# Re-planned issue order in a multi-query attention kernel: earlier value products, planned value scalings, another start and end

## The chip, the cores and the metric

The kernel runs on one core of a Trainium2 chip. The metric is the device time of one execution in microseconds (us). TensorE is called PE here, its weight loads PEld, VectorE is DVE, ScalarE is ACT, GpSimd is POOL and SyncE is SP. The program has one core, so there is no second die to compare with.

## The reference, cut to what matters

```python
batch, seq_len, embed_dim = (8, 1024, 1024); num_heads = 16; head_dim = 64
# q: (8, 1024, 16, 64), k and v: (8, 1024, 64): one key and value head for all query heads
scores = np.matmul(q, k.transpose(0, 1, 3, 2)) / np.sqrt(head_dim)
weights = np.exp(scores - np.max(scores, axis=-1, keepdims=True))
weights = weights / np.sum(weights, axis=-1, keepdims=True)
attn_out = np.matmul(weights, v)
```

## The kernel before

The work is cut into 64 pairs of heads (8 per batch), and a pair into 8 key tiles of 128 keys. A key tile has two halves of 512 queries. For each half, PE makes scores for both heads (a "score product", two matmuls), then one engine turns them into weights, then PE multiplies weights and values (the "value products").

The exponential is the expensive part, and two engines share it. ACT does most tiles, one instruction of 128x1024 per half. Some tiles go to DVE, which builds the exponential from bit operations and products as a sum of three terms: two instructions `z` (one per half) and four further steps per tile. The three terms need three copies of the values, scaled by constants ("value scalings", three DVE instructions per batch). A DVE tile therefore also costs PE three times the value products.

What each engine does next is decided when the kernel is built. A function `plan` simulates PE, ACT and DVE with a handful of durations and emits the order of operations, which the program then follows. These are its constants, and the parts that the change touches (`...` marks a cut; most comments are added here):

```python
ACT_P, ACT_L = 0.905, 1.19                 # pace and latency of one ACT exponential, us
MARGIN, WAIT = 0.318, 0.153
END, END_LAG = 2.388, -0.293
BACKLOG, BACK_END = 4.816, 2.496           # how much DVE work may be open for one more DVE tile
LAST, SPLIT = 10, 3                        # no DVE tile in the last 10; the last 3 go half by half
WBUFS = 26
ZBUFS = 5
LAG = 1.355                                # value products trail scores by this many pairs
...
            lag = min(LAG, END_LAG + (LAG - END_LAG) * rest / END)
            av = tav <= T + (SWITCH if mode != "av" else 0) and (
                nv < 3 * NKT * (nq / (2 * NKT) - lag) or nq == 2 * NT
            )
...
    def begin(w):                          # called with the first score product of pair w
        ...
        if w == 1:
            scale_v(0)                     # three DVE instructions that plan() knows nothing of
        ...
            if hp == HP - 3:
                trans_k(b + 1)
                scale_v(b + 1)
...
        turn_first(0)                      # first halves of the first keys and queries, transposed on PE
        for n, (_, _, (op, *args)) in enumerate(order):
            if n == 2:
                turn_first(1)              # second halves, after two score products
            if op == "qk":
                ...
                score(*args)
```

The softmax here doesn't subtract the row's maximum and nothing guards it: scores larger than these inputs give would overflow.

## Time and profile before

The median of the first three runs is 763.41 us (763.12 to 763.8).

| | before |
|---|---|
| exponentials on ACT, pace | 812, 0.917 us |
| start of the first, end of the last | 7.01 us, 755.56 us |
| time lost in gaps between them | 4.15 us |
| from there to the end of the span | 5.70 us |

The pace is the median distance between the ends of successive exponentials in the trace. "Time lost in gaps" is the sum of what these distances exceed 0.9165 us by, over the 14 that do so by more than 0.025 us. With 1.02 us for the first exponential alone, 811 x 0.9165 = 743.3 us for the others and the rows of the table, 7.01 + 1.02 + 743.3 + 4.15 + 5.70 adds to 761.2 us of a span of 761.27 us. This sum is the budget in which the change is judged.

The page of the kernel before starts with the span and with busy time by engine (share of the span, number of instructions).

```profile
span 761.3 us, 29601 instructions
PE 731.3 (96%) x13648; PEld 485.3 (64%) x13648; DVE 728.3 (96%) x1050; ACT 747.6 (98%) x814; POOL 44.6 (6%) x61
```

ACT is the busiest, but PE and DVE are close, so a busy share alone does not settle which one bounds. Three of the groups of instructions of the same page follow. The columns are line, engine, operation, output and input, count, then busy time, mean ns of one, then idle time just before them and what ended most of it.

```profile
L432 ACT ACTIVATE w<-sc 128x1024 f16<-128x1024 f32 x812 | 745.7, 1295 | 3.8 <-PE sc L420 3.3
L446 DVE TENSOR_SCALAR z<-sc 128x1024 uint16<-128x1024 f32 x212 | 258.4, 1219 | 13.3 <-PE sc L420 10.1
L328 DVE TENSOR_SCALAR vals<-vn 128x512 f16<-128x512 f32 x24 | 8.7, 419 | 0.0
```

An exponential lasts 1.3 us on average in the record but they follow each other every 0.917 us, because neighbours overlap. The timeline of ACT of the kernel before shows the idle stretches; the columns are start, duration of the merged stretch, what ran, and in brackets the idle time before it and who ended it.

```profile
7.01 1.02 ACT L432 ACTIVATE w<-sc 128x1024 f16<-128x1024 f32 x1 [0.97 <-PE sc L420]
9.10 12.94 ACT L432 ACTIVATE w<-sc 128x1024 f16<-128x1024 f32 x14 [1.07 <-PE sc L420]
22.55 1.02 ACT L432 ACTIVATE w<-sc 128x1024 f16<-128x1024 f32 x1 [0.51 <-PE sc L420]
23.85 3.03 ACT L432 ACTIVATE w<-sc 128x1024 f16<-128x1024 f32 x3 [0.28 <-PE sc L420]
27.31 728.25 ACT L432 ACTIVATE w<-sc 128x1024 f16<-128x1024 f32 x793 [0.43 <-PE sc L420]
```

After 27.3 us the stretch of 793 exponentials looks unbroken, but the ends of single instructions show six losses of 0.13 to 0.25 us hidden in it and three smaller ones, 1.25 us together. Around 22 us the timelines of DVE and PE say who was late. First DVE:

```profile
19.02 1.09 DVE L328 TENSOR_SCALAR vals<-vn 128x512 f16<-128x512 f32 x3
20.03 0.69 DVE L459 TENSOR_SCALAR m<-z 128x2048 uint16<-128x2048 uint16 x1
20.63 1.22 DVE L446 TENSOR_SCALAR z<-sc 128x1024 uint16<-128x1024 f32 x1
```

Then PE, where score matmuls and the first value matmuls alternate:

```profile
21.90 1.03 PE L420 MATMUL sc<-qt,k2t 64*128 64x512 f16 x4 [1.03 <-DVE z L446]
22.87 0.40 PE L476 MATMUL acc<-vals,w 128*128 128x65 f16 x4
23.20 0.61 PE L420 MATMUL sc<-qt,k2t 64*128 64x512 f16 x2
25.58 0.52 PE L476 MATMUL acc<-vals,e 128*128 128x65 f16 x6
```

PE waited 1.03 us for the DVE exponential that stood behind the scalings. Besides, PE was slow here: score matmuls last about 0.6 us until 24.7 us, and 0.386 us later (median from 26.7 to 39.7 us). The trace, asked for the score line from 6.3 to 26.4 us, gives the shortest, median and longest in ns:

```profile
L420 PE MATMUL sc<-qt,k2t x50: 580/604/631, 6.4 to 24.7; 64*128 64x512 f16 x50
```

The trace's record of the granted clock begins only at 26.44 us, with the full clock, and the first fast score matmul starts at 26.67 us. So this phase is called PE's slow clock here, and its end the release. The granted-clock row does not show it: it reads 1.00 for 7 to 28 us of the kernel before, where score matmuls lasted 604 ns until 24.7 us. The matmul durations do.

### The profile page before, as it was taken

How to read it: one execution, taken by the hardware profiler on the slowest of the kernel's cores; microseconds unless marked ns; L12 is line 12 of the kernel's file. 1: busy time of each engine (PE TensorE's matmuls, PEld its weight loads, DVE VectorE, ACT ScalarE, POOL GpSimd, SP SyncE). 2: the span in 40 equal slices, each digit the busy share in tenths (PEclk: the TensorE clock that was granted, in tenths of full speed). 3: DMA queues.
4: the chain of work that ended last, by engine and by line, in shares of the span. 5: the costliest groups of instructions: out<-in, count | busy, mean ns of one | idle time of the engine just before them, and what ended most of it. 6: DMA issues, size and time to landing. Idle time of an engine off the chain costs nothing.

```text
span 761.3 us, 29601 instructions
## 1 busy us (share of the span) xinstructions
PE 731.3 (96%) x13648; PEld 485.3 (64%) x13648; DVE 728.3 (96%) x1050; ACT 747.6 (98%) x814; POOL 44.6 (6%) x61
## 2 busy tenths in 40 slices
PE   5999999999999999999999999999999999999997
PEld 1565666666666666665666666666666666666666
DVE  5999999999999999999999999999999999999993
ACT  6999999999999999999999999999999999999997
POOL 2100010000100001000010000100001000000000
PEclk9999999999999999999999999999999999999999
DMA  7945566545763449544397544756348454431323
GB/s 115 144 91 99 112 92 107 113 88 96 105 120 85 86 98 141 102 87 98 66 121 134 85 106 74 117 113 123 67 97 109 98 107 91 101 82 45 85 58 84
DMA packets 189836, 75.04 MB, mean 99 GB/s; under 512 B 90256, under 2 KB 188560, under 8 KB 189712
## 3 DMA queue, kind: packets, MB, share of 16 engines
q1 hardware_dynamic: 140544, 54.14, 32.1%
q0 software_dynamic: 47840, 18.35, 21.0%
q8 instruction: 106, 1.74, 0.9%
q10 hardware_dynamic: 1328, 0.66, 0.3%
q14 instruction: 18, 0.15, 0.1%
HBM read 39.58 MB, written 33.55 MB: 96 GB/s over the span
## 4 chain that ended last, share of the span: by engine, by line
ACT 81%; PE 9%; DVE 8%; issue 1%; DMA 0%; POOL 0%; DVEq 0%
ACT w L432 81%; PE acc L476 5%; PE sc L420 4%; DVE z L446 3%; DVE m L462 1%; DVE m L463 1%; DVE vals L328 1%; DVE osb L498 1%; DVE m L459 1%; DVE e L456 1%; DMA kn<-in_k_dram 0%; DVE rec L489 0%; PE qps L403 0%; POOL k L378 0%; DVE qt L412 0%
## 5 line engine op out<-in xcount | busy, mean ns | idle before, releaser
L432 ACT ACTIVATE w<-sc 128x1024 f16<-128x1024 f32 x812 | 745.7, 1295 | 3.8 <-PE sc L420 3.3
L420 PE MATMUL sc<-qt,k2t 64*128 64x512 f16 x2048 | 349.3, 388 | 19.9 <-ACT w L432 10.9
L476 PE MATMUL acc<-vals,w 128*128 128x65 f16 x6496 | 315.7, 194 | 1.2 <-DVE osb L498 0.9
L476 PEld LDWEIGHTS <-w 128*128 128x128 f16 x6496 | 242.0, 97 | 88.3 <-issue 85.7
L446 DVE TENSOR_SCALAR z<-sc 128x1024 uint16<-128x1024 f32 x212 | 258.4, 1219 | 13.3 <-PE sc L420 10.1
L420 PEld LDWEIGHTS <-k2t 64*128 64x128 f16 x2048 | 99.0, 93 | 98.5 <-issue 48.0
L462 DVE TENSOR_TENSOR m<-m 128x2048 f16<-128x2048 f16 x106 | 128.3, 1210 | 0.4
L463 DVE TENSOR_TENSOR m<-z,m 128x2048 f16<-128x2048 f16 x106 | 127.8, 1206 | 0.1
L476 PE MATMUL acc<-vals,e 128*128 128x65 f16 x1696 | 115.3, 194 | 0.0
L476 PE MATMUL acc<-vals,z 128*128 128x65 f16 x1696 | 114.5, 194 | 0.0
L476 PE MATMUL acc<-vals,m 128*128 128x65 f16 x1696 | 110.8, 194 | 0.0
L498 DVE TENSOR_TENSOR osb<-acc,rec 128x384 f32<-128x384 f32 (+1 forms) x192 | 96.3, 503 | 0.3
L476 PEld LDWEIGHTS <-m 128*128 128x128 f16 x1696 | 74.0, 97 | 30.9 <-issue 28.4
L476 PEld LDWEIGHTS <-e 128*128 128x128 f16 x1696 | 76.3, 97 | 25.1 <-issue 25.1
L476 PEld LDWEIGHTS <-z 128*128 128x128 f16 x1696 | 76.0, 97 | 23.3 <-issue 23.3
L456 DVE TENSOR_SCALAR e<-z 128x2048 uint16<-128x2048 uint16 x106 | 73.0, 688 | 0.1
L459 DVE TENSOR_SCALAR m<-z 128x2048 uint16<-128x2048 uint16 x106 | 71.8, 678 | 0.0
L352 POOL DMA_DIRECT2D qn<-in_q_dram x32 | 29.6, 926 | 615.9 <-DMA qt<-qn 613.9
L489 DVE RECIPROCAL rec<-acc 128x6 f32<-128x6 f32 (+1 forms) x192 | 34.1, 180 | 9.1 <-PE acc L476 9.1
L313 POOL DMA_DIRECT2D k<-in_k_dram x14 | 12.7, 914 | 0.0
L328 DVE TENSOR_SCALAR vals<-vn 128x512 f16<-128x512 f32 x24 | 8.7, 419 | 0.0
L398 PE MATMUL kps<-ident,k 128*128 128x128 f16 x8 | 1.2, 311 | 4.8 <-POOL k L378 4.8
(19 smaller groups left out, 9.8 us busy)
## 6 DMA issues: line engine op xcount, KB each, us to landing
out_dram<-osb SPq DMA_DIRECT2D x63, 512.0 KB, 3.8
qn<-in_q_dram POOLq DMA_DIRECT2D x31, 512.0 KB, 5.8
vn<-in_v_dram SPq DMA_DIRECT2D x8, 256.0 KB, 2.8
k<-in_k_dram POOLq DMA_DIRECT2D x14, 128.0 KB, 5.9
qf<-in_q_dram ACTq DMA_DIRECT2D x2, 256.0 KB, 4.1
qt<-qn SPq DMA_TRANSPOSE x32, 4.8
out_dram<-osb SPq DMA_DIRECT2D x2, 192.0 KB, 2.1
kn<-in_k_dram SPq DMA_DIRECT2D x1, 256.0 KB, 3.1
```

Of the source, the lines that this page charges most:

```text
L328: nc.vector.tensor_scalar(out=x[:, :, 0:D], in0=st["vn"], scalar1=c, scalar2=None, op0=ALU.mult)
L352: nc.gpsimd.dma_start(out=qn[ps[0]].rearrange("p (c r) x -> p c (r x)", r=len(ps)), in_=q[b, :, 2 * hp : 2 * hp + 2 * len(ps), :].rearrang ...
L420: nc.tensor.matmul(sc[t, c][:, h, :], kst[p // HP]["k2t"][64 * h : 64 * h + 64, j, :], qt[p][64 * h : 64 * h + 64, 4 * c : 4 * c + 4, :], ...
L432: ins = nc.scalar.activation(out=w, in_=sc.pop((t, c)), func=EXP, scale=ascale).ins
L446: nc.vector.tensor_scalar(out=z[:, :, c * QC : (c + 1) * QC], in0=sc.pop((t, c)), scalar1=vscale, scalar2=(15 + math.log2(C0)) * ONE, op0= ...
L456: lambda: V.tensor_scalar(out=wt[t].bitcast(U16), in0=z, scalar1=0xFC00, scalar2=None, op0=ALU.bitwise_and),
L459: lambda: V.tensor_scalar(out=m.bitcast(U16), in0=z, scalar1=1023, scalar2=14 << 10, op0=ALU.bitwise_and, op1=ALU.bitwise_or),
L462: lambda: V.tensor_tensor(out=m, in0=m, in1=m, op=ALU.mult),
L463: lambda: V.tensor_tensor(out=m, in0=z.bitcast(FP16), in1=m, op=ALU.mult),
L476: nc.tensor.matmul(acc[p, grp][:, o : o + D + 1], w[:, h, i * P : (i + 1) * P], kst[p // HP]["v"][k][:, j, 0 : D + 1], start=(n == 0 and y ...
L489: nc.vector.reciprocal(out=rec[p, grp][:, 0 : a.shape[1]], in_=a[:, :, D])
L498: nc.vector.tensor_tensor(out=o.rearrange("p i (h d) -> p (i h) d", h=2)[:, BLOCKS[grp] : BLOCKS[grp + 1], :], in0=a[:, :, 0:D], in1=rec.p ...
```

## The change

The intent is to take out the gaps and to move a little more work off ACT. The diff, cut to its core (some retuned constants and the bookkeeping of the new order are left out, and comments are added):

```diff
-ACT_P, ACT_L = 0.905, 1.19
+ACT_P, ACT_L = 0.9167, 1.19
-MARGIN, WAIT = 0.318, 0.153
-END, END_LAG = 2.388, -0.293
-VEC = dict(z=1.13, rec=0.11)
+MARGIN, WAIT = 0.295, 0.162
+END, END_LAG = 4.363, 0.69
+VEC = dict(z=1.13, rec=0.11, val=0.34)
-BACKLOG, BACK_END = 4.816, 2.496
-LAST, SPLIT = 10, 3
-WBUFS = 26
-ZBUFS = 5
+BACKLOG, BACK_END = 6.82, 5.788
+LAST, SPLIT, FIRST = 10, 4, 3
+RAMP, VALS, COLD, WARM = 0.395, 3.0, 2, 9.0
+WBUFS = 23
+ZBUFS = 6
 ...
+    vals = [(VALS, 0, k) for k in range(len(TERMS))]      # scalings become planned DVE work
+    vdone: dict = {}
 ...
+            if nt // NKT >= HP * nb - 3 and nb * HP < NP:
+                vals += [(T, nb, k) for k in range(len(TERMS))]
+            cold = COLD if T < WARM else 1                # PE planned at half speed at first
 ...
-            lag = min(LAG, END_LAG + (LAG - END_LAG) * rest / END)
+            lag = min(LAG, END_LAG + (LAG - END_LAG) * rest / END, RAMP * nq / (2 * NKT))
 ...
-        if w == 1:
-            scale_v(0)
-                scale_v(b + 1)
 ...
-            if n == 2:
-                turn_first(1)
+                if scores in (3, 7):                      # queries after 3 scores, keys after 7
+                    turn_first(1 if scores == 3 else 2)
+                if scores == 9:                           # value products may start
+                    while held:
+                        value(*held.pop(0))
```

`FIRST = 3` lets the first three ACT tiles use the first query half one after the other, so that three scores need no second transposes. In the two builds' instruction lists DVE has 107 tiles instead of 106, ACT 810 exponentials instead of 812, and PE 32 value matmuls more.

More of the change, by code (lines that the diff above doesn't have):

```diff
@@ L30 @@
 VEC_DEP = 0.12
-BACKLOG, BACK_END = 4.816, 2.496
-LAST, SPLIT = 10, 3
-WBUFS = 26
-ZBUFS = 5
-LAG = 1.355
+BACKLOG, BACK_END = 6.82, 5.788
[3 more added lines that the diff above has]
+ZBUFS = 6
+LAG = 1.341
 FAR = 1e9
@@ L40, in follows @@
 def follows(x, y):
-    if y is None or len(x) != len(y) and y[0] != "z":
+    if y is None:
         return False
     if len(x) == 5:
-        return x[1] == "norm" and y[1] == "rec" and x[2:] == y[2:]
-    if len(x) != 2:
+        return len(y) == 5 and x[1] == "norm" and y[1] == "rec" and x[2:] == y[2:]
+    if len(x) != 2 or len(y) != 2:
         return False
@@ L50, in follows, with plan @@
     return x[0] == y[0] and (x[1], y[1]) in ((2, 1), (3, 2))
-def plan(NP, NKT):
+def plan(NP, NKT, HP=8):
     NT = NP * NKT
@@ L70, in plan @@
     nq = nv = 0
-    nt, units, vunits = 0, [], []
+    nt, units, vunits, nb = 0, [], [], 1
     gap = 99
@@ L107, in plan @@
                     nt += 1
-                aring += range(nt, nt + 1 if nt < NT - SPLIT else NT)
-                if nt < NT - SPLIT:
-                    ring.append(nt)
-                    units = [(nt, 0), (nt, 1)]
-                    nt += 1
-                else:
-                    ring += range(nt, NT)
-                    units = [(t, c) for c in range(2) for t in range(nt, NT)]
-                    nt = NT
+                n = NT if nt >= NT - SPLIT else nt + 1 if nt > 1 else nt + FIRST
+                aring += range(nt, n)
+                ring += range(nt, n)
+                units = [(t, c) for c in range(2) for t in range(nt, n)]
+                nt = n
+            if nt // NKT >= HP * nb - 3 and nb * HP < NP:
+                vals += [(T, nb, k) for k in range(len(TERMS))]
+                nb += 1
+            cold = COLD if T < WARM else 1
             free = [s for s in range(3) if slot[s] <= T + (SWITCH if mode != "qk" else 0)]
@@ L142, in plan @@
                         r = max(ready.get((t, c), FAR) for c in ((0,), (0, 1), (1,))[gg])
+                    r = max(r, vdone.get((gp // HP, k), FAR))
                     if n == 0:
@@ L147, in plan @@
             rest = (2 * NT - nq) / (2 * NKT)
-            lag = min(LAG, END_LAG + (LAG - END_LAG) * rest / END)
-            cost = AV_B * STEP
+            lag = min(LAG, END_LAG + (LAG - END_LAG) * rest / END, RAMP * nq / (2 * NKT))
+            cost = AV_B * STEP * cold
             av = tav <= T + (SWITCH if mode != "av" else 0) and (
@@ L170, in plan @@
                 st = max(T + (SWITCH if mode != "qk" else 0), slot[s])
-                pe, mode = st + QK_P, "qk"
+                pe, mode = st + QK_P * cold, "qk"
                 nq += 1
@@ L175, in plan @@
                     slot[s] = FAR
-                    zs.append((st + PE_L, s, u))
+                    zs.append((st + PE_L + QK_P * (cold - 1), s, u))
                     gap = 0
@@ L179, in plan @@
                     u = units.pop(0)
-                    act = max(act, st + PE_L)
+                    act = max(act, st + PE_L + QK_P * (cold - 1))
                     emit(act, "act", *u)
@@ L209, in plan @@
             todo = [("ev", x) for x in evs if x[0] <= T]
+            todo += [("val", x) for x in vals if x[0] <= T][:1]
             todo += [("step", x) for x in steps if x == min(y for y in steps if y[0] == x[0])][:2]
@@ L234, in plan @@
                 last = x
+            elif what == "val":
+                vals.remove(x)
+                emit(T, "val", *x[1:])
+                dve = T + VEC["val"]
+                vdone[x[1:]] = dve + VEC_L
+                last = None
             elif what == "step":
@@ L242, in plan @@
             else:
-                nxt = [x[0] for x in zs + evs if x[0] > T] + [pe + 1e-6] * (pe > T)
+                nxt = [x[0] for x in zs + evs + vals if x[0] > T] + [pe + 1e-6] * (pe > T)
                 dve = max(min(nxt, default=0.0), T + 1e-3)
@@ L292 @@
     wbuf = [consts.tile([P, 2, S], FP16, name=f"w{i}") for i in range(WBUFS)]
-    order, vtiles = plan(NP, NKT)
+    order, vtiles = plan(NP, NKT, HP)
     writers: dict = {}
@@ L305 @@
     rec: dict = {}
+    rec_made: set = set()
     osb: dict = {}
@@ L321, in load_v, with scale_v @@
         nc.sync.dma_start(out=st["vn"], in_=v[b].rearrange("(p c) d -> p c d", p=P))
-    def scale_v(b):
-        st = kst[b]
-        st["v"] = vals[b % 2]
-        for x, c in zip(st["v"], TERMS):
-            nc.vector.tensor_scalar(
-                out=x[:, :, 0:D], in0=st["vn"], scalar1=c, scalar2=None, op0=ALU.mult)
+    def scale_v(b, k):
+        kst[b]["v"] = vals[b % 2]
+        nc.vector.tensor_scalar(
+            out=vals[b % 2][k][:, :, 0:D], in0=kst[b]["vn"], scalar1=TERMS[k], scalar2=None,
+            op0=ALU.mult)
     def trans_k(b):
@@ L385, in load_first, with turn_first @@
         qt[0] = queries(qtp, "qt", 0, 1)
-    def turn_first(c):
+    def turn_first(n):
         st = kst[0]
-        x = slice(4 * c, 4 * c + 4)
-        if c == 0:
+        if n == 0:
             st["k2t"] = kvp.tile([P, NKT + 1, P], FP16, tag="k2t", name="k2t0")[:, 0:NKT, :]
@@ L395, in turn_first @@
             nc.vector.tensor_copy(out=st["k16"][:, :, 0, :], in_=st["kn"])
-        ks, qs = [
-            [
-                lambda i=i: nc.tensor.transpose(st["kps"][:, i, :], st["k16"][
-                    :, i, :, :].rearrange("p r d -> p (r d)"), ident)
-                for i in range(4 * c, 4 * c + 4)
-            ],
-            [
-                lambda i=i: nc.tensor.transpose(st["qps"][:, i, :], qn[0][:, i, :], ident)
-                for i in range(4 * c, 4 * c + 4)
-            ],
-        ]
-        nc.vector.tensor_copy(out=qn[0][:, x, :], in_=st["qf"][:, x, :])
-        for f in ks + qs if c == 0 else qs + ks:
-            f()
-        if c == 0:
-            nc.scalar.copy(out=st["k2t"][:, x, :], in_=st["kps"][:, x, :])
-        nc.vector.tensor_copy(out=qt[0][:, x, :], in_=st["qps"][:, x, :])
-        if c == 1:
-            nc.vector.tensor_copy(out=st["k2t"][:, x, :], in_=st["kps"][:, x, :])
+        half = range(4 * min(n, 1), 4 * min(n, 1) + 4)
+        x = slice(half[0], half[-1] + 1)
+        if n == 0:
+            nc.vector.tensor_copy(out=qn[0][:, x, :], in_=st["qf"][:, x, :])
+        if n != 1:
+            for i in half:
+                nc.tensor.transpose(
+                    st["kps"][:, i, :], st["k16"][:, i, :, :].rearrange("p r d -> p (r d)"), ident)
+            copy = nc.scalar.copy if n == 0 else nc.vector.tensor_copy
+            copy(out=st["k2t"][:, x, :], in_=st["kps"][:, x, :])
+        if n < 2:
+            for i in half:
+                nc.tensor.transpose(st["qps"][:, i, :], qn[0][:, i, :], ident)
+            nc.vector.tensor_copy(out=qt[0][:, x, :], in_=st["qps"][:, x, :])
+        if n == 0:
+            nc.vector.tensor_copy(out=qn[0][:, 4:8, :], in_=st["qf"][:, 4:8, :])
     def score(t, c, s):
@@ L487, in reciprocal @@
         a = blocks(p, grp)
+        rec_made.add((p, grp))
         rec[p, grp] = recp.tile([P, 8], FP32, tag="rec", name=f"rec{p}_{grp}")
@@ L494, in normalise @@
         n = a.shape[1]
-        if grp == 0:
+        if p not in osb:
             osb[p] = osbp.tile([P, NKT, 2 * D], FP32, tag="osb", name=f"osb{p}")
@@ L506, in normalise @@
             i0, i1 = BLOCKS[grp] // 2, BLOCKS[grp + 1] // 2
-        elif grp == 2:
+        elif not any((p, x) in acc or (p, x) not in rec_made for x in range(3)):
             i0, i1 = 0, NKT
@@ L543 @@
         trans_q(1)
-        for n, (_, _, (op, *args)) in enumerate(order):
-            if n == 2:
-                turn_first(1)
+        scores, held = 0, []
+        for _, _, (op, *args) in order:
             if op == "qk":
+                if scores in (3, 7):
[3 more added lines that the diff above has]
+                        value(*held.pop(0))
+                scores += 1
                 while begun <= args[0] // NKT:
@@ L555 @@
                 exp_dve(*args)
+            elif op == "val":
+                scale_v(*args)
             elif op == "step":
                 steps[args[0]][args[1]]()
+            elif op == "av" and scores <= 9:
+                held.append(args)
             elif op == "av":
```

## The prediction

> **What bounds the kernel now.** ScalarE (ACT). The busy table gives ACT 747.6 of 761.3 us (98%). [...]in ACT's timeline the 812 exponentials start at 7.01 us and end at 755.56 us. Their ends are a median 0.917 us apart; the excess over that sums to about 4 us. So the span is 7.0 before the first exponential + 1.0 for it + 811 x 0.917 + about 4 of gaps + 5.7 after the last one. PE and DVE are at 96% each, but hardly hold ACT up.
>
> **Where ACT's gaps are** (ACT timeline):
> - 8.02 to 9.10 us: the third score product waits behind the second half of the query/key transposes.
> - 22 to 27.3 us, four gaps, about 1.7 us of excess: the value products begin at 22.87 us with PE still slow. Score matmuls last 0.58 to 0.63 us until 26.4 us and 0.38 us afterwards; value matmuls are spaced 55 ns, then 30 ns. [...] The three value scalings (1.09 us of DVE at 19.02 us) add to it: PE waits 1.03 us for a DVE exponential just after.
> - About seven gaps of 0.1 to 0.25 us later (70, 164, 257, 441, 442, 532 us): most follow one of the value scalings, 1.0 us of DVE that the planner did not know of.
>
> **What the change does.** The issue orders of the two builds show:
> 1. One more key tile goes to DVE (107 instead of 106): two exponentials fewer on ACT, -1.83 us, and six DVE instructions more. By the groups' mean durations DVE gains 6.2 us (728 to 734), and PE 1 us (32 value matmuls at 30 ns). DVE idles 33 us today, so this should fit.
> 2. The start: three first-half scores precede the second transposes, so the 1.1 us gap at 8 us nearly goes: -1.0.
> 3. Value products start after the ninth score (about 12 us instead of 22.9). PE warms up some 9 us earlier, and the slow clock is planned for: the four gaps at 22 to 27 us go, perhaps 0.3 new: -1.4.
> 4. Value scalings are placed by the planner: -0.8 of the late gaps.
> 5. The end: 26 pairs of value matmuls rather than 24 after the last exponential, four tiles split instead of three: +0.1 us.
>
> All of this lies on ACT's chain, except the added PE and DVE work. Sum: -4.9 us, 763.4 to 758.5 us. Range 757.0 to 761.0.
>
> **What would show it.** Right: 810 exponentials, still 0.917 us apart; first one still at 7.0 us; no ACT gap over 0.4 us; score matmuls at 0.38 us from about 16 us on; ACT busy about 745.8; 5.8 us after the last exponential. A step is wrong if its gap is still there, or the count or spacing differs.
>
> **What would make it wrong.** The old plan assumed 0.905 us per exponential, so PE and DVE had 1.3% slack against the real 0.917; the new one plans 0.9167, with one more DVE tile. If DVE or PE then delivers scores late, many small ACT gaps appear in the steady part and eat the gain. A clock that releases later than planned would leave stalls near 13 to 17 us. Chances: faster by over 2% 0.01, within 2% 0.98, slower 0.01.

-1.83 - 1.0 - 1.4 - 0.8 + 0.1 makes -4.9 us. The fast scores "from about 16 us on" are the estimate from the trace of the kernel before: there the scores became fast 3.5 us after the first value product (22.87 and 26.4 us), and that product was to move to about 12 us.

## The result, and the profile after

The changed kernel ran in 758.52 us (median of 10 runs, 757.95 to 759.42), the kernel before in 763.07 us (12 runs, 762.63 to 763.89). The ratio is 0.9939 with a 95% interval of 0.993 to 0.9948. The profiled run took 757.97 us, one of the fastest of the ten, so the two profiles differ by 5.21 us where the medians differ by 4.55 us.

The span and busy times of the changed kernel:

```profile
span 756.1 us, 29670 instructions
PE 722.2 (96%) x13680; PEld 485.0 (64%) x13680; DVE 730.8 (97%) x1056; ACT 744.9 (99%) x812; POOL 44.9 (6%) x61
```

The same three groups:

```profile
L441 ACT ACTIVATE w<-sc 128x1024 f16<-128x1024 f32 x810 | 743.1, 1306 | 1.1 <-PE sc L429 1.0
L455 DVE TENSOR_SCALAR z<-sc 128x1024 uint16<-128x1024 f32 x214 | 260.6, 1218 | 7.0 <-PE sc L429 3.5
L339 DVE TENSOR_SCALAR vals<-vn 128x512 f16<-128x512 f32 x24 | 9.4, 428 | 0.0
```

The timeline of ACT has one stretch where there were five:

```profile
7.03 743.24 ACT L441 ACTIVATE w<-sc 128x1024 f16<-128x1024 f32 x810 [0.96 <-PE sc L429]
```

The score line of the changed kernel, asked from 6 to 9.7 us and shown here as that view gives it: the last slow matmul starts at 9.5 us, instead of 24.7 us.

```profile
L429 PE MATMUL sc<-qt,k2t x12: 582/610/631, 6.4 to 9.5; 64*128 64x512 f16 x12
```

PE's timeline shows when the value products begin, and that the scores were already fast by then (0.39 us for two):

```profile
10.96 0.39 PE L429 MATMUL sc<-qt,k2t 64*128 64x512 f16 x2 [0.19 <-ACT w L441]
12.06 0.39 PE L429 MATMUL sc<-qt,k2t 64*128 64x512 f16 x2 [0.71 <-DVE k2t L417]
12.39 0.42 PE L485 MATMUL acc<-vals,w 128*128 128x65 f16 x8
```

The chain that ended last, by engine, of the kernel before:

```profile
ACT 81%; PE 9%; DVE 8%; issue 1%; DMA 0%; POOL 0%; DVEq 0%
```

and of the changed one, where hardly anything but ACT is left on it:

```profile
ACT 95%; PE 3%; DVE 1%; DMA 0%; issue 0%; POOL 0%
```

The budget of the span, worked out from both traces, accounts for the whole difference of 5.21 us. It has to, because the gaps are defined as what exceeds 0.9165 us; what it shows is that the pace stayed the same and where the rest lies:

| part of ACT's chain | before | after | difference | predicted |
|---|---|---|---|---|
| start of the first exponential | 7.01 | 7.03 | +0.02 | 0 |
| exponentials after the first, at 0.9165 us | 743.3 | 741.4 | -1.83 | -1.83 |
| gaps before 15 us | 1.18 | 0.34 | -0.84 | -1.0 |
| gaps from 15 to 40 us | 1.72 | 0.20 | -1.52 | -1.4 |
| gaps after 40 us | 1.25 | 0.11 | -1.14 | -0.8 |
| after the last exponential | 5.70 | 5.79 | +0.09 | +0.1 |
| sum | | | -5.22 | -4.9 |

### The profile page after: what moved, and what is told of

The parts are those of the page before. It is cut to its first block, busy times and chain, and to the rows that moved or that the text cites. A ratio compares the mean times of both kernels' runs of the same rounds, so it can differ in the third digit from the quotient of the medians.

```text
span 756.1 us, 29670 instructions
## 1 busy us (share of the span) xinstructions
PE 722.2 (96%) x13680; PEld 485.0 (64%) x13680; DVE 730.8 (97%) x1056; ACT 744.9 (99%) x812; POOL 44.9 (6%) x61
## 4 chain that ended last, share of the span: by engine, by line
ACT 95%; PE 3%; DVE 1%; DMA 0%; issue 0%; POOL 0%
ACT w L441 95%; PE acc L485 2%; PE sc L429 1%; DVE z L455 1%; DMA kn<-in_k_dram 0%; DVE m L472 0%; DVE m L471 0%; POOL k L390 0%; DVE qt L421 0%; PE kps L414 0%; DVE m L468 0%; DVE e L465 0%; DVE osb L508 0%; PE qps L420 0%; DVE vals L339 0%
## 5 line engine op out<-in xcount | busy, mean ns | idle before, releaser
L429 PE MATMUL sc<-qt,k2t 64*128 64x512 f16 x2048 | 341.3, 383 | 23.3 <-ACT w L441 16.8
L485 PE MATMUL acc<-vals,w 128*128 128x65 f16 x6480 | 308.9, 193 | 0.5 <-DVE osb L508 0.3
L485 PEld LDWEIGHTS <-w 128*128 128x128 f16 x6480 | 238.8, 97 | 90.5 <-issue 89.5
L485 PE MATMUL acc<-vals,e 128*128 128x65 f16 x1712 | 118.3, 194 | 0.6 <-DVE osb L508 0.4
L485 PE MATMUL acc<-vals,z 128*128 128x65 f16 x1712 | 112.5, 193 | 0.0
L485 PE MATMUL acc<-vals,m 128*128 128x65 f16 x1712 | 106.4, 194 | 0.6 <-DVE m L472 0.5
L485 PEld LDWEIGHTS <-m 128*128 128x128 f16 x1712 | 72.8, 97 | 25.4 <-issue 24.1
```

The costliest lines, as they stand in the source:

```text
L429: nc.tensor.matmul(sc[t, c][:, h, :], kst[p // HP]["k2t"][64 * h : 64 * h + 64, j, :], qt[p][64 * h : 64 * h + 64, 4 * c : 4 * c + 4, :], ...
L485: nc.tensor.matmul(acc[p, grp][:, o : o + D + 1], w[:, h, i * P : (i + 1) * P], kst[p // HP]["v"][k][:, j, 0 : D + 1], start=(n == 0 and y ...
```

## The experiments

The bookkeeping says where the time went, not which part of the change did it. The theory: ACT's chain sets the time, each part of the change shortens its own term, and the gaps at 22 us come from PE's slow clock together with the scalings. The rivals: the scalings alone make these gaps; or PE or DVE, both at 96%, set the time somewhere. All twelve runs gave correct results.

**1. The kernel before with PE kept busy.** Four transposes after each of the score products 4 to 21, into a tile that nobody reads:

```diff
                 score(*args)
+                if n > 2 and asked < 18:
+                    asked += 1
+                    for i in range(4):
+                        nc.tensor.transpose(warm[:, i, :], ident, ident)
```

> The kernel before, with four extra 128x128 transposes of the identity after each of the next eighteen score products, written to a tile nobody reads; nothing else moves. Theory (PE's slow clock causes ACT's gaps between 22 and 27 us): the extra work releases the clock before the value products begin, so score matmuls last about 0.38 us by 20 us instead of 0.6, and the excess of 1.7 us between 22 and 27.3 us falls to 0.6 or less; time about 1.2 us below the kernel before. Rival (the value scalings on DVE at 19 us cause them): PE is fast by then, but the gaps stay at about 1.7 us and the time is unchanged or higher. The gap of 1.2 us at 8 to 9 us stays in both cases.

Measured: 763.38 us, ratio to the kernel before 0.9997 (0.9985 to 1.0009). The score matmuls were fast from 13.1 us on (372 to 388 ns until 23.8 us). In the timeline of ACT the gaps of 22 to 27 us shrink to one:

```profile
9.09 2.85 ACT L432 ACTIVATE w<-sc 128x1024 f16<-128x1024 f32 x3 [1.07 <-PE sc L420]
12.85 11.16 ACT L432 ACTIVATE w<-sc 128x1024 f16<-128x1024 f32 x12 [0.91 <-PE sc L420]
24.18 508.23 ACT L432 ACTIVATE w<-sc 128x1024 f16<-128x1024 f32 x553 [0.16 <-PE sc L420]
```

The loss from 15 to 40 us fell from 1.72 to 0.48 us, as the slow-clock theory said. The time missed its expectation, because the extra transposes themselves held up a score product: a new gap of 0.91 us at 12 us (a loss of 1.02 us) gave back most of it.

**2. The kernel before with the first scalings moved.**

```diff
-        if w == 1:
-            scale_v(0)
...
+            if n == 5:
+                scale_v(0)
```

> The kernel before, with the three value scalings of the first batch moved on DVE from 19 us to 10 us, where DVE waits 1.1 us today. Rival theory (scalings cause the gaps): the gap of 0.62 us at 22.0 to 22.6 us goes and most of the rest of the 1.7 us too, time 1 to 1.5 us lower. Slow-clock theory: at most the first gap (0.6 us) goes, since PE waited for a DVE exponential just before it; the three gaps from 23.6 to 27.3 us (1.1 us together) stay, because the value matmuls still start at 55 ns spacing.

Measured: 762.32 us, ratio 0.9982 (0.997 to 0.9994). By the ratio that is 1.4 us lower (0.5 to 2.3), which is the time that the scalings theory expected, but the two profiled spans differ by 0.69 us only, so the time doesn't decide between the theories and the gaps have to. In its timeline of ACT the first two gaps are gone, and the last one is larger than the 0.43 us before:

```profile
9.17 16.79 ACT L432 ACTIVATE w<-sc 128x1024 f16<-128x1024 f32 x18 [1.07 <-PE sc L420]
26.63 728.26 ACT L432 ACTIVATE w<-sc 128x1024 f16<-128x1024 f32 x793 [0.68 <-PE sc L420]
```

The loss from 15 to 40 us was 0.96 us. So neither cause is alone: without the scalings 0.76 us of 1.72 goes, with a fast PE 1.24 us; together they would be 2.0, so they overlap. The score matmuls of this trace stayed slow until 25.9 us.

**3. The changed kernel without the ramp.**

```diff
-RAMP, VALS, COLD, WARM = 0.395, 3.0, 2, 9.0
+RAMP, VALS, COLD, WARM = 9.9, 3.0, 2, 9.0
```

> The changed kernel without the ramp: value products start at the full lag again, after 22 scores (about 22 us). If the early start of the value products is what releases PE's clock early, score matmuls stay at 0.6 us until about 26 us, and ACT's gaps between 22 and 27 us come back with 1 us or more. If the clock is released for another reason (in the changed kernel's profile it was released at 10.0 us, before its first value product at 12.4 us), score matmuls are at 0.38 us from about 10 us again and no gap over 0.3 us appears there. In both cases 59 instead of 26 pairs of value matmuls stand after the last exponential, so the tail is about 2 us longer (33 x 2 x 30 ns): time about 2 to 3.5 us above the changed kernel.

Measured: 760.95 us, ratio 0.9966 (0.9953 to 0.9979), 2.1 us above the changed kernel by the ratios. What happened was neither branch of the expectation. The scores became fast at 10.9 us, and slow again from 14.4 to 22.8 us, as the trace says of its score line between 14.3 and 22.9 us:

```profile
L429 PE MATMUL sc<-qt,k2t x24: 579/606/631, 14.4 to 22.8; 64*128 64x512 f16 x24
```

Three losses of 0.46, 0.28 and 0.29 us came back from 18 to 25 us, and 2.5 us were added after the last exponential (8.31 instead of 5.79 us; 2.0 expected). So here the scores became fast without value products, and without them they were slow again; in the changed kernel, which had value products from 12.39 us, score matmuls stayed at 372 to 387 ns from 11.0 to 25.5 us. All five runs of this kernel have a mean clock of 0.992 to 0.996, against 0.997 to 1.000 in the ten of the changed kernel.

**4. The changed kernel with the old start.**

```diff
-LAST, SPLIT, FIRST = 10, 4, 3
+LAST, SPLIT, FIRST = 10, 4, 1
...
-                if scores in (3, 7):
-                    turn_first(1 if scores == 3 else 2)
+                if scores == 2:
+                    turn_first(1)
+                    turn_first(2)
```

> The changed kernel with the old start: both halves of the second transposes after two scores, one key tile at a time. Theory: the gap of about 1.1 us after the first exponential returns, so the time is about 0.8 us above the changed kernel; nothing else changes by over 0.3 us. Rival (the early gap is hidden by what follows, because PE or DVE bound the start): time unchanged.

Measured: 759.66 us, ratio 0.9954 (0.9943 to 0.9966), about 1.1 us above the changed kernel by the ratios. In the timeline of ACT the old gap is back, but there are others:

```profile
9.04 5.61 ACT L441 ACTIVATE w<-sc 128x1024 f16<-128x1024 f32 x6 [1.06 <-PE sc L429]
15.12 14.22 ACT L441 ACTIVATE w<-sc 128x1024 f16<-128x1024 f32 x15 [0.48 <-PE sc L429]
29.81 1.02 ACT L441 ACTIVATE w<-sc 128x1024 f16<-128x1024 f32 x1 [0.46 <-PE sc L429]
```

The gap of 0.48 us at 15 us falls into the slow clock of the start (score matmuls of 0.61 us until 17.4 us here); it was not expected. The gap at 29 us comes with a lower granted clock. The table by stretches, for 27 to 38 us (columns: busy time of PE, PEld, DVE, ACT and POOL, then the granted clock, the DMA share and GB/s), shows this:

```profile
27.00:38.00 11.00, 10.38 (x164) 6.24 (x160) 9.93 (x16) 9.91 (x11) 0.21 (x1) 0.84 1.06 138
```

The granted clock was 0.84 in these 11 us. It was 0.84 again from 165 to 176 us, against 1.00 from 160 to 165 us. ACT lost 1.5 and 1.2 us around these two slow stretches. The profiled run took 762.18 us; the other five took 759.13 to 759.92 us. The expected 0.8 us fits those five: against the kernel before in the same rounds they are 0.7 us slower than the changed kernel.

**5 and 6. One DVE tile fewer, and one more.**

```diff
-LAST, SPLIT, FIRST = 10, 4, 3
+LAST, SPLIT, FIRST = 14, 4, 3      # 106 DVE tiles
+LAST, SPLIT, FIRST = 8, 4, 3       # 108 DVE tiles, in the other run
```

> The changed kernel with no DVE tile among the last fourteen: 106 tiles on DVE and 812 exponentials on ACT, as in the kernel before. Theory (ACT bounds): the exponentials end 1.83 us later; 14 instead of 26 pairs of value matmuls follow the last one, which takes 0.7 us off the tail (12 x 2 x 30 ns): time 1.1 us above the changed kernel. Rival (PE's or DVE's end bounds): time unchanged or lower.

> The changed kernel with one tile more on DVE near the end: 108, so 808 exponentials. If only the count of exponentials matters: 1.83 us below the changed kernel. Theory (ACT bounds until its last exponential, PE after it): the exponentials end 1.8 us earlier, but 66 instead of 26 pairs of value matmuls follow the last one, +2.4 us of tail (40 x 2 x 30 ns): time 0.6 us above the changed kernel, so the limit of this trade is reached. DVE as the limit would show as gaps of ACT that wait for scores behind DVE exponentials in the last 30 us.

Measured with 106: 759.8 us, ratio 0.9953 (0.994 to 0.9965), 1.1 us above the changed kernel by the ratios. In the profile the exponentials end at 752.10 us, 1.83 us later, and the tail is 5.07 us, 0.72 us shorter. Both terms are as expected.

Measured with 108: 759.04 us, ratio 0.9948 (0.9935 to 0.996). The exponentials end at 749.29 us, with an early loss of 1.37 us, 1.03 us more than in the changed kernel's profile, most of it at 14.8 us, before the scores became fast in this run (16.8 us, see run 9). All its losses together are 0.85 us more than the changed kernel's; without these 0.85 us the exponentials would end 1.83 us earlier, as expected. But the tail grows to 8.53 us, by 2.74 us. The end of PE and DVE in its timeline:

```profile
749.55 4.14 PE L485 MATMUL acc<-vals,w 128*128 128x65 f16 x128
753.96 0.56 DVE L508 TENSOR_TENSOR osb<-acc,rec 128x384 f32<-128x384 f32 x1
```

The same place in the changed kernel, where fewer value matmuls are left over:

```profile
749.83 2.19 PE L485 MATMUL acc<-vals,w 128*128 128x65 f16 x61
752.28 0.56 DVE L508 TENSOR_TENSOR osb<-acc,rec 128x384 f32<-128x384 f32 x1
```

So in both directions the exchange is worth what the pace says, and beyond 107, in this plan, PE takes it back at the end. The timing intervals of both runs overlap with the changed kernel's; the profiles carry this verdict.

**7. The changed kernel with unplanned scalings.** From the second batch on:

```diff
-                vals += [(T, nb, k) for k in range(len(TERMS))]
+                for k in range(len(TERMS)):
+                    vdone[nb, k] = T
...
                 trans_k(b + 1)
+                for k in range(len(TERMS)):
+                    scale_v(b + 1, k)
```

(with `LAST = 13`, which keeps 107 DVE tiles)

> The changed kernel, but from the second batch on the value scalings stand where they stood before (three in a row when a pair of heads begins, unknown to the planner); 107 tiles on DVE, 27 pairs of value matmuls after the last exponential, as in the changed kernel. Theory: ACT gaps of 0.1 to 0.3 us return after most of the seven groups of scalings, 0.8 us or more in total against 0.1; time 0.8 us above the changed kernel. Rival (the late gaps went because of other tuned constants): late excess stays under 0.3 us.

Measured: 764.33 us, ratio 1.0008 (0.9995 to 1.0022). The expectation of 0.8 us was far too small: by the median the whole gain of the change is gone. Part of that is the clock: four of the five runs have a mean clock of 0.995 to 0.998, and the fifth, with 0.999, took 762.18 us, 3.7 us above the changed kernel. Some of the gaps in its timeline of ACT:

```profile
66.62 43.27 ACT L442 ACTIVATE w<-sc 128x1024 f16<-128x1024 f32 x47 [0.39 <-PE sc L430]
111.62 50.74 ACT L442 ACTIVATE w<-sc 128x1024 f16<-128x1024 f32 x55 [0.40 <-PE sc L430]
253.08 91.92 ACT L442 ACTIVATE w<-sc 128x1024 f16<-128x1024 f32 x100 [0.30 <-PE sc L430]
351.36 184.03 ACT L442 ACTIVATE w<-sc 128x1024 f16<-128x1024 f32 x200 [0.47 <-PE sc L430]
```

The loss after 40 us was 6.33 us. Seven groups, each 2 to 10 us behind one of the seven scalings (62.8, 156.5, 250.5, 342.4, 437.9, 529.6 and 622.6 us), make 3.6 us of it, 0.4 to 0.6 us each. That they are due to the scalings is read from this order in time. The losses near 111 and 351 us coincide with two slow stretches of the clock in the trace and make 2.7 us: from 109.5 to 111.4 us six score matmuls lasted 574 to 607 ns, against a median of 386 ns from 113.0 us on. The rest of this run's extra time is the late release at the start (16.8 us; 1.0 us lost) and a longer tail (0.4 us).

**8. The same, planned with the old pace.** Why does the same omission cost 3.6 us here and at most 1.25 us in the kernel before?

```diff
-ACT_P, ACT_L = 0.9167, 1.19
+ACT_P, ACT_L = 0.905, 1.19         # 106 DVE tiles
```

> The run with unplanned value scalings again, but planned with the old pace of 0.905 us per exponential: 106 tiles on DVE and 812 exponentials, as in the kernel before, so PE and DVE have 1.3% of slack against the real pace again. In the run with 0.9167 us and 107 tiles the seven groups of scalings cost ACT 3.6 us of gaps (0.4 to 0.6 each, two slow stretches of the clock not counted). Theory (the same scalings cost more there because the slack was gone): here 1.5 us or less, as in the kernel before (1.25). Rival (the cost comes from the other constants, such as the margin or the buffers): about 3.6 us again. 65 pairs of value matmuls stand after the last exponential, so the time itself, about 762, says little; the gaps decide.

Measured: 764.46 us, ratio 1.0007 (0.9991 to 1.0024), with a tail of 8.36 us. The loss after 40 us was 2.84 us, of which 1.13 us lie at a slow stretch of the clock (206 us; the run's mean clock is 0.996). The remaining 1.7 us is a little more than the 1.5 us expected, and half of the 3.6 us of run 7. So most of the difference is the slack which an optimistic pace and one tile fewer leave on PE and DVE. Pace and tile count were changed together, so their shares stay open.

**9. The changed kernel again, and with PE kept busy before the keys arrive.**

```diff
+        warm = psp.tile([P, NKT, P], FP16, tag="acc1", name="warm")
+        for i in range(28):
+            nc.tensor.transpose(warm[:, i % NKT, :], ident, ident)
         turn_first(0)
```

> The changed kernel once more, beside the two that follow and to see how far the moment of the clock's release moves in it: in runs with the same start, score matmuls became fast at 10.0, 11.0, 12.1 and twice 16.8 us. Time 758.0 to 759.4 us. If the release is late (about 16.8 us), ACT has a gap of about 1.2 us near 14.8 us; if early, none over 0.3 us.

> The changed kernel with 28 transposes of the identity on PE from about 1.6 to 4.8 us, while PE waits for the first keys; the result is not used. Theory ([...]the slow start costs ACT 0.3 to 1.3 us): score matmuls are fast by 8.5 us at the latest, the early excess of ACT falls to 0.2 us or less in the profile, the first exponential starts up to 0.2 us earlier, no gap near 14.8 us; time 0.3 to 1.0 us below the changed kernel of the same rounds, with a smaller spread. Rival (the release follows a phase that this work doesn't move): fast at some time between 10 and 17 us as before, time unchanged.

The run tests whether work on PE before the keys arrive makes the scores fast earlier.

Measured, changed kernel again: 758.44 us, ratio 0.9939 (0.9927 to 0.9951), scores fast at 9.5 us. Over the profiles whose start is the changed kernel's (the scaling runs included), the moment was 9.5, 10.0, 10.0, 11.0, 12.1 and twice 16.8 us. In both runs with 16.8 us ACT lost 1.16 us at 14.8 us; in none of the others did it lose over 0.25 us there.

Measured with the transposes: 758.02 us (757.03 to 761.26), ratio 0.9938 (0.9924 to 0.9953). PE's timeline shows them, and the first score products, three of which now take 0.82 us instead of 1.46:

```profile
1.57 3.17 PE L550 MATMUL warm<-ident 128*128 128x128 f16 x28 [1.57 <-POOL ident masks.py:199]
6.65 0.82 PE L429 MATMUL sc<-qt,k2t 64*128 64x512 f16 x6 [0.52 <-DVE qt L421]
```

No score matmul was slow (372 to 387 ns from 6.6 to 19.6 us), and ACT had no visible loss in the whole run: 0 instead of 0.48 us in the repeat. The median is 0.4 us lower, inside the expectation, but the ratio does not tell the two apart. The spread did not shrink: the slowest run, 761.26 us, has the lowest mean clock of these six (0.994, the others 0.997 to 1.000).

**10. A shorter end, alone and with these transposes.**

```diff
-MARGIN, WAIT = 0.295, 0.162
-END, END_LAG = 4.363, 0.69
+MARGIN, WAIT = 0.295, 0.1717
+END, END_LAG = 5.102, -0.418
-BACKLOG, BACK_END = 6.82, 5.788
-LAST, SPLIT, FIRST = 10, 4, 3
-RAMP, VALS, COLD, WARM = 0.395, 3.0, 2, 9.0
+BACKLOG, BACK_END = 6.803, 1.744
+LAST, SPLIT, FIRST = 5, 5, 3
+RAMP, VALS, COLD, WARM = 0.3505, 3.0, 2, 9.0
-LAG = 1.341
+LAG = 1.476
```

> The changed kernel with other planner constants for the end (five tiles split instead of four, DVE tiles until the last five, lag falling further): still 107 DVE tiles and 810 exponentials, but 5 instead of 26 pairs of value matmuls after the last exponential. Expected: value matmuls end about 1.26 us earlier (21 x 2 x 30 ns), but two groups are then normalised one after the other at the very end (+0.6 us): time 0.6 us below the changed kernel. If the last output transfer sets the end regardless, unchanged. If the tighter end starves ACT, gaps in the last 60 us.

> Both at once: the planner constants for the shorter end (0.7 us off the tail) and the transposes that keep PE busy before the first keys. If the two gains lie at different ends of ACT's chain, they add: 1.0 to 1.7 us below the changed kernel, about 757 us; faster than both kernels.

Measured, shorter end alone: 757.97 us, ratio 0.9929 (0.9916 to 0.9941); the tail is 5.08 instead of 5.79 us. Its profile lost 0.66 us at a slow stretch of the clock (25.4 to 27.6 us; the run's mean clock is 0.998). Both together: 757.17 us (756.23 to 758.21), ratio 0.9921 (0.9909 to 0.9934), 1.3 us below the changed kernel of the same rounds. This is the lowest median measured here and clearly below the kernel before; its interval still touches the changed kernel's. In its profile a new wait appears, in the list of waits from 24 to 33 us:

```profile
PE sc L429 <- DMA qt<-qn: 1.1, 1, 1.1
```

The transposed queries of the third pair landed at 28.3 us, when PE had been ready for them for 1.1 us; ACT lost 0.92 us in the 4 us that followed. In the changed kernel they landed at 25.0 us, before PE came to them; their transfer was issued at 17.4 us there and at 22.2 us here.

## Why the prediction was right or wrong

The predicted time, 758.5 us, was met (758.52 us). That it was met to 0.02 us is luck: the forecast took 4.9 us off 763.4 us, the median of the first three runs, while the medians of all runs differ by 4.55 us (from 763.07 us) and the profiles by 5.21 us. That it was met within half a microsecond is not: no term of the budget is off by over 0.35 us.

- *What bounds the kernel.* ACT's chain. ACT was busy for 98% of the span before and 99% after, and its share of the last chain rose from 81% to 95%. Runs 5 and 6 confirm the exchange rate of 1.83 us for two exponentials.
- *Step 1, two exponentials fewer, -1.83 us.* Right. The side terms were mis-sized, off the chain: DVE busy rose by 2.5 us (728.3 to 730.8), not 6.2, and PE busy fell by 9.1 us instead of rising by 1. For DVE, adding mean durations counts twice what neighbours overlap: the durations of all its instructions add to 803.0 us before and 807.8 us after, for busy times of 728.3 and 730.8 us. Why PE's fell was not traced. Fewer slow matmuls may be a part: from 7 to 28 us, PE was busy for 17.7 us with 218 matmuls, and for 17.1 us with 116 in the kernel before.
- *Step 2, the start, -1.0 us.* Right, measured -0.84; run 4 shows that the new start does it.
- *Step 3, the gaps at 22 us, -1.4 us.* The size was right (-1.52), the mechanism half wrong. "PE warms up some 9 us earlier" was to follow from value products at about 12 us, with fast scores "from about 16 us on". The scores were fast at 10.0 us, before the first value product. In run 3, without value products at this point, they were slow again from 14.4 to 22.8 us. In two runs with the same start (6 and 7) the scores became fast at 16.8 us, near the predicted time; that the value products did it there is not shown. Run 1 confirms that a fast PE takes away most of these gaps (1.24 of 1.72 us), and run 2 that the scalings have a part.
- *Step 4, planned scalings, -0.8 us.* Measured -1.14 in the budget. The larger error is in what this part means: taken out of the new kernel it costs 3.6 us in gaps of ACT, mostly because the new plan has no slack left for it (with the old pace, and so one tile fewer, 1.7 us; runs 7 and 8).
- *Step 5, the end, +0.1 us.* Right, +0.09.
- *The named risks.* Small gaps in the steady part did not come (0.11 us after 40 us). The clock's moment does vary as feared, 9.5 to 16.8 us, and costs up to 1.2 us, which is part of the spread from 757.95 to 759.42 us.

Why is the clock released at 10 us in one start and at 26 us in another? The table by stretches gives, in this order, the changed kernel just before its release (9.93 us), and for the kernel before the same stretch, the time after it and the stretch just before its own release (stretch and its length, then busy time of PE, PEld, DVE, ACT and POOL, granted clock, DMA share and GB/s):

```profile
7.00:9.90 2.90, 2.76 (x14) 0.75 (x11) 2.44 (x4) 2.87 (x4) 1.12 (x1) 1.00 1.07 129
7.00:9.90 2.90, 2.40 (x14) 1.00 (x12) 1.84 (x3) 1.82 (x2) 0.87 (x1) 1.00 0.97 105
9.90:23.50 13.60, 10.23 (x42) 2.34 (x42) 12.36 (x16) 13.09 (x15) 0.87 (x1) 1.00 0.99 130
23.50:26.40 2.90, 2.90 (x35) 1.73 (x34) 2.90 (x4) 2.54 (x4) 1.42 (x2) 1.00 0.40 120
```

PE was busy for 95%, 83%, 75% and 100% of them. In these two traces the release followed a stretch with a busier PE, in the kernel before only with its value products. With four transposes added per score product (run 1) the scores were fast from 13.1 us on, and with 28 transposes beforehand (run 9) from the first one, at 6.65 us.

What stays open: how busy PE has to be, and for how long, was not tested by a run, and the same start gave 9.5 to 16.8 us. Nor is it shown what makes the clock fall in mid-program.

## What to carry to other kernels

When one engine runs at 98%, write the time as a sum along that engine (start, count times pace, gaps, tail), take each number from the ends of single instructions, and judge every part of a change by its own term. A static plan with exact durations runs without gaps only if every instruction of the busy engines is in it: three forgotten DVE instructions per batch cost twice as much in the tight plan as in the loose one (3.6 and 1.7 us, runs 7 and 8). Work moved off the bound engine has to fit the end of the program too, where another engine finishes.
